# Streamed weights in DRAM by half units, and other SBUF offsets for half of the q/k weight tiles

## The chip, the cores and the metric

The kernel runs on one core of one Trainium2 chip. The metric is the device time of one execution in microseconds (us), from outside the span that the profiler records; three executions were timed, and the profile comes from another one.

## The reference, cut to what matters

One decoder block over 256 tokens of 2048 channels, in float32. Almost all of its work is products of the 256 tokens with large weight matrices:

```python
proj = x @ w_in                                   # 2048 x 13336
gq, gk, gv, gr, glr, fq, fk, fv, ff, ma, mb = jnp.split(proj, offsets, axis=-1)
q = gq.reshape(B, S, GLA_HEADS, GLA_DK) * (GLA_DK ** -0.5)
k = gk.reshape(B, S, GLA_HEADS, GLA_DK)
...
o = gla_chunked(q, k, v, log_a)                   # gated linear attention
of = fox_attention(fqh, fkh, fvh, log_f)          # softmax attention, 8 heads of 128
merged = jax.nn.sigmoid(ma) * (o @ w_branch_gla) + jax.nn.sigmoid(mb) * (of @ w_branch_fox)
x = layer_norm(ALPHA * x + merged @ w_out)
h = jax.nn.gelu(causal_dwconv(x @ w_gate)) * (x @ w_up)       # 5632 wide
x = layer_norm(ALPHA * x + h @ w_down)
x = x + jax.nn.sigmoid(x @ w_ple_gate) * (p @ w_ple_proj)
```

The change touches how the weights of these products lie in DRAM, and where the weights of `fq`, `fk`, `gq` and `gk` lie in SBUF.

## The kernel before, in words

**Units.** All large weights are laid out on the host as one tensor `wu` of units. A unit is 128 partitions x 2048 floats (1 MB) and is streamed as two halves of 128 x 1024 floats (512 KB). Units 0 to 15 are the softmax attention's q and k (`psfq`, `psfk` in the trace, one unit each in turn), 16 to 31 the linear attention's (`psq`, `psk`, two units each in turn), 32 to 135 the merge gates, v, output gate, branches and output projection, 136 to 223 the MLP's gate and up (`psg`, `psu` in turn), and the rest the down projection and the last gate.

**Precision.** A float32 product is made of three products of rounded operands: each weight half `raw` is split into `hi` (ScalarE, `copy`, L130) and `lo = raw - hi` (VectorE, L255). The activations are split likewise and lie side by side, 256 columns each.

**A q/k or gate/up unit** (`w_unit`, L314 to L342) gives 128 output channels. It runs over 16 blocks of 128 input channels. For each block it loads 128 x 128 of `hi` as weights and multiplies by 512 columns of activations (L320), then loads 128 x 128 of `lo` and multiplies by 256 columns (L325). Such a *pair* of matmuls stands 16 times in a unit. The first eight pairs take their weights from the tiles of the first half, the last eight from those of the second. In units 0 to 31 a callback (`tick`) runs after the eighth pair: it may put matmuls of the attention (`psg` L582, `pl` L622, transposes, `po`, `pa`) between the two halves. In the gate/up stage there is none, and every 14th unit (`TURN`) takes its last ten pairs in another order.

In the other stages `hi` and `lo` are the moving operand, not the weights of TensorE.

**Tiles and their offsets.** `hi` and `lo` rotate through six buffers each. A buffer has 1088 floats a partition (4352 bytes, 17 x 256), of which 1024 are used, from an offset that `place(u)` gives in floats. Both pools begin at a multiple of 256 bytes, and so do the activations `xT` and `x1T`; the offset alone sets the address modulo 256. For units 0 to 31 and the gate/up units it is 16 for `hi` and 4 for `lo` (64 and 16 bytes); for the TURN units 0 and 60 (0 and 240 bytes); elsewhere 0 and 0, but for three units.

**Streams.** SyncE issues each half's load (L251 in `prep`, L210 and L214 in `prep_s`) some three units ahead of its use, through five `raw` buffers. A unit that `park_gen` takes is loaded whole (L191), VectorE forms differences of it, GpSimd's queue writes them to the DRAM tensor `td`, and `prep_s` reads them back in a later stage. In DRAM the unit's row of 2048 floats (8 KB) of a partition is contiguous, so a half's load reads 128 runs of 4 KB, 8 KB apart.

The order of the matmuls, the splits and the loads is the program's, apart from the priorities of a scheduler; the queue of SyncE is in program order.

Of the kernel before, what the change touches and what calls it, by code (L numbers as in the profile page):

```python
# [19 lines left out]
P = 128  # L20
# [16 lines left out]


TURN = range(139, 224, 14)


def place(u):
    if 32 <= u < 136 or u >= 224:
        return 0, 0
    if 136 <= u < 139:
        return 0, 16
    return (0, 60) if u in TURN else (16, 4)


P_STAT = 5000  # L50
# [37 lines left out]
def tile_block(ctx: ExitStack, tc: tile.TileContext, wu, wfv, wpp, xT_in, x_in, pT_in, wlr,  # L88
               chan, gnorm, lng, ident_in, mask_in, cmask_in, out):
    nc = tc.nc  # L90
# [23 lines left out]
    def s8(shape, dt=F32, name=None):  # L114
        return big.tile(shape, dt, tag="S8", name=name)

    def t1(name):
        return sm.tile([P, 256], F32, tag="t1", bufs=6, name=name)
# [10 lines left out]
    def copy(o, i, scale=1.0):  # L129
        return nc.scalar.activation(o, i, AF.Copy, bias=0.0, scale=scale)  # L130
# [29 lines left out]
    hS = {}  # L160

    def lo_tile(u, name):
        o = place(u)[1]
        return rlo.tile([P, 1088], F32R, tag="lo", name=f"lo{name}")[:, o:o + 1024]

    def hi_tile(u, name):
        o = place(u)[0]
        return rhi.tile([P, 1088], F32R, tag="hi", name=f"hi{name}")[:, o:o + 1024]

    def differences(r0, r1, h, pinned=False):  # L170
# [11 lines left out]
    def park(w, i):  # L182
        for h in range(2):
            differences(w[:, 0:1024], w[:, 1024:2048], h, h == 0)
        nc.gpsimd.dma_start(td[i], w)

    def park_gen(units, lag, rest):

        for u in units:
            w = s8([P, 2048], name=f"td{parked[u]}")  # L190
            nc.sync.dma_start(w, wu[u])  # L191
            for _ in range(lag):
                yield
            park(w, parked[u])
            n = parked[u] - parked[units[0]]
            for _ in range(rest[n % len(rest)] if isinstance(rest, tuple) else rest):
                yield

    def prep_s(u):


        r0, r1 = [ring.tile([P, 1024], F32, tag="raw", bufs=5, name=f"raw{u}_{h}")
                  for h in range(2)]
        b12, b11, b22, b21 = r0[:, 0:512], r0[:, 512:1024], r1[:, 0:512], r1[:, 512:1024]
        rt = (r0, r1)
        if u in parked:
            nc.sync.dma_start(b11, wu[u, :, 512:1024])
            nc.sync.dma_start(r1, wu[u, :, 1024:2048])
            w = s8([P, 2048], name=f"td{u}")
            nc.sync.dma_start(w, td[parked[u]])  # L210
            rt = (w[:, 0:1024], w[:, 1024:2048])
        else:
            for h, r in enumerate((r0, r1)):
                nc.sync.dma_start(r, wu[u, :, h * 1024:(h + 1) * 1024])  # L214
        if dn0 <= u < dn0 + NF:
            nh = (u - dn0) // (NF // 2)
            pair = DN_ORDER[nh][(u - dn0) % (NF // 2)]
            i = DN_S[0].index(pair)
            if i % 2 == 0:
                two = s8([P, 8, 256], F32R, name=f"hS{nh}_{pair}")  # L220
                nc.sync.dma_start(two.bitcast(F32), sd[i // 2].rearrange(
                    "p (i n) -> p i n", i=8))
                hS[nh, pair], hS[nh, DN_S[0][i + 1]] = two[:, 0:4], two[:, 4:8]

        def split(src, name, e=slice(0, 1024)):
            hi = hi_tile(u, f"{u}_{name}")[:, e]
            lo = lo_tile(u, f"{u}_{name}")[:, e]
            copy(hi, src)
            nc.vector.tensor_tensor(lo, src, hi.bitcast(F32), ALU.subtract)  # L229
            return [(hi[:, o:o + 512], lo[:, o:o + 512]) for o in range(0, src.shape[1], 512)]  # L230

        x11, = split(b11, "b11", slice(512, 1024))
        x22, x21 = split(r1, "b2")
        if u not in parked:
            differences(r0, r1, 0)
        t3, t1_ = split(rt[0], "t13")
        if u not in parked:
            differences(r0, r1, 1)
        t2_, t4 = split(rt[1], "t24")
        ready[u] = [x11, x21, x22, t1_, t3, t2_, t4]  # L240

    def prep(pinned=False):
        u = n_prep[0]
        n_prep[0] += 1
        if u in s_units:
            prep_s(u)
            return
        his, los = [], []
        for h in range(2):
            raw = ring.tile([P, 1024], F32, tag="raw", bufs=5, name=f"raw{u}_{h}")  # L250
            nc.sync.dma_start(raw, wu[u, :, h * 1024:(h + 1) * 1024])  # L251
            hi = hi_tile(u, f"{u}_{h}")
            copy(hi, raw)
            lo = lo_tile(u, f"{u}_{h}")
            i = nc.vector.tensor_tensor(lo, raw, hi.bitcast(F32), ALU.subtract)  # L255
            if pinned:
                tc.keep_in_program_order(i)
            his.append(hi)
            los.append(lo)
        ready[u] = (his, los)  # L260
# [53 lines left out]
    def w_unit(ps, hi, lo, act, kts, first, last, tick=None):  # L314
# [13 lines left out]

        turn = n_used[0] - 1 in TURN
        pairs = 6 if turn else n  # L330
# [155 lines left out]
    for u in range(8):  # L486
        hi, lo = fvu[u]
        for j in range(2):
# [8 lines left out]
            for t, i, c in seq:  # L497
                o, n = fch[c]
                w, x = prods[t][i]
# [34 lines left out]
    for t in range(2):  # L534
        for c, (o, n) in enumerate(fch):
            n = min(n, 1024 - o)
# [143 lines left out]
    for n in range(16):  # L680
        h, j = n // 2, n % 2
# [115 lines left out]
    for n in range(16):  # L797
        nm, dst, sc = (("q", gq, 1.0 / 16.0), ("k", gk, 1.0))[n // 2 % 2]
        h, c = n // 4, n % 2
# [648 lines left out]
    for n in range(NF):  # L1448
# [18 lines left out]
        u = t1("up")  # L1467
# [4 lines left out]
        if pair in DN_S[0]:  # L1472
            if j == 0:
                yp = t2("yp").rearrange("p (k t) -> p k t", t=S)
            h = yp[:, j, :]
        else:
            h = y
# [4 lines left out]
        if pair in DN_S[0] and j == 1:  # L1482
            v = s_sums(yp)
            for i in range(2):
                w = sm.tile([P, 2, 256], F32R, tag="t2", bufs=6, name="hs")
# [4 lines left out]
                o = k % 2 * 1024 + 512 * i  # L1490
# [215 lines left out]
def _sst(w, orders, ssets):  # L1706


    out = []
    for nh, (order, sset) in enumerate(zip(orders, ssets)):  # L1710
        for n in order:
            b = [[w[(2 * n + j) * P:(2 * n + j + 1) * P,
                    nh * 1024 + c * 512:nh * 1024 + c * 512 + 512] for c in range(2)]
                 for j in range(2)]
            out.append(np.concatenate([b[0][1], b[0][0], b[1][1], b[1][0]] if n in sset
                                      else b[0] + b[1], 1))
    return np.stack(out)


def _fold(a):  # L1720

    return np.concatenate([a[:P], a[P:][::-1]], 0)
# [6 lines left out]
def _layout(i):  # L1729
    w_in = i["w_in"][0]  # L1730
    c = lambda nm, n: w_in[:, OFF[nm]:OFF[nm] + n]
    bg, bf = _qst(i["w_branch_gla"][0]), _qst(i["w_branch_fox"][0])
    br = [w for q in range(4) for w in (bg[4 * q:4 * q + 4], bf[2 * q:2 * q + 2])]
    gu = np.stack([_wst(i["w_gate"][0]), _wst(i["w_up"][0])], 1).reshape(2 * NF, P, 2048)
    qk = np.stack([_wst(c(n, 1024)).reshape(4, 2, P, 2048) for n in ("gq", "gk")], 1)
    m = np.concatenate([_qst(c(n, 2048)) for n in ("ma", "mb")], 0)
    wu = np.concatenate(
        [np.stack([_wst(c("fq", 1024)), _wst(c("fk", 1024))], 1).reshape(16, P, 2048), qk.reshape(16, P, 2048), m[:PSM1],
         _sst(c("gv", 2048), GV_ORDER, GV_S), _sst(c("gr", 2048), GV_ORDER, GR_S), m[PSM1:]] + br
        + [_sst(i["w_out"][0], OUT_ORDER, WO_S), gu,  # L1740
           _sst(i["w_down"][0], DN_ORDER, DN_S),
           _sst(i["w_ple_gate"][0], PG_ORDER, PG_S)], 0)
    wfv = np.concatenate([c("fv", 1024), c("glr", 16), c("ff", 8)], 1)
    wfv = wfv.reshape(8, 2, P, NS).transpose(0, 2, 1, 3)
    x = _fold(i["x"][0])
    bfo = np.zeros((P, 1), np.float32)
    bfo[:FH, 0] = i["b_forget"][0]
    chan = np.concatenate(
        [_chan(i["b_gla_lr"][0]), bfo, _chan(i["ln1_g"][0]), _chan(i["ln1_b"][0]),
         _chan(i["ln2_g"][0]), _chan(i["ln2_b"][0])]  # L1750
        + [_chan(i["conv_w"][0][j]) for j in range(3)] + [_chan(i["conv_b"][0])], 1)
    lng = np.stack([i["ln1_g"], i["ln1_b"], i["ln2_g"], i["ln2_b"]])
    s = np.arange(P)[:, None]
    t = np.arange(P)[None, :]
    masks = [s == t]
    for lev in range(1, 8):
        L = 1 << lev
        masks.append((s // L == t // L) & (s % L < L // 2) & (t % L >= L // 2))
    mask = np.stack([m if h == 0 else m.T for m in masks for h in range(2)], 1).astype(np.float32)
    caus = np.where(t <= s, 0.0, NEG).astype(np.float32)  # L1760
    cmask = np.concatenate([caus.T, caus], 1)
    return dict(wu=wu, wfv=wfv, wpp=_xst(i["w_ple_proj"][0]), xT=x.T.reshape(16, P, S).transpose(1, 0, 2),
                x=x.reshape(2, P, D), pT=_fold(i["p"][0, 0]).T.reshape(2, P, S).transpose(1, 0, 2),
                wlr=i["w_gla_lr"][0], chan=chan, gnorm=i["gla_norm_g"], lng=lng,
                ident=np.eye(P, dtype=np.float32), mask=mask, cmask=cmask)
# [20 lines left out]
```

## Time and profile before

| | |
|---|---|
| three timed executions | 1636.01 us median (1635.70 to 1637.37) |
| the profiled execution | 1635.61 us, of which the span 1633.8 us |
| TensorE matmuls, busy | 1627.3 us of the span, 8422 instructions |
| VectorE, busy | 1343.7 us |
| ScalarE, busy | 933.6 us |
| SyncE's DMA queue | 417.57 MB, 72.0% of the 16 engines' span |
| GpSimd's DMA queue | 58.73 MB, 9.0% |

How to read it: a busy share of TensorE near 100% says that matmuls stood in the array all the time, not that they ran at one rate. A matmul's recorded duration is longer than its share of the time, since matmuls are pipelined; the rate is read from the distance between the starts of successive matmuls.

### The profile page before, as it was taken

The page shows a single profiled execution, that of the slowest core. Times are in us where ns is not written, and L with a number is a line of the kernel's source. Part 1 is how long each engine was busy: PE and PEld are TensorE (multiplying, and loading weights), DVE is VectorE, ACT ScalarE, POOL GpSimd, SP SyncE. Part 2 cuts the span into 40 slices and gives each one's busy share as a digit, 9 for nine tenths or more (in the row PEclk, how much of TensorE's full clock was granted, in tenths as well). Part 3 has the DMA queues.
Part 4 walks back from the last instruction along what each step waited for, and adds up shares of the span by engine and source line. Part 5 has one row for each costly group of instructions (what it writes and reads, how often), then busy time and mean ns, then how long its engine had stood idle before and what let it go on. Part 6 is the DMA issues. An engine that isn't in the chain of part 4 may idle for free.

```text
span 1633.8 us, 23487 instructions
## 1 busy us (share of the span) xinstructions
PE 1627.3 (100%) x8422; PEld 1395.0 (85%) x8422; DVE 1343.7 (82%) x1920; ACT 933.6 (57%) x1321; POOL 93.0 (6%) x244
## 2 busy tenths in 40 slices
PE   9999999999999999999999999999999999999998
PEld 8988888888888888888898888888888888888887
DVE  7698899788989867879986887888777688988887
ACT  6655555456666653546575554665555555556554
POOL 0000000000000000000010111111110000000000
PEclk9999999999999999999999999999999999999999
DMA  9799899878898758889856887989776688899574
GB/s 328 286 371 340 295 388 352 294 261 305 305 349 299 250 191 322 299 321 389 300 187 198 323 309 284 350 305 357 280 239 222 201 285 326 305 351 355 168 261 152
DMA packets 114838, 477.81 MB, mean 292 GB/s; under 512 B 13032, under 2 KB 14320, under 8 KB 95136
## 3 DMA queue, kind: packets, MB, share of 16 engines
q1 hardware_dynamic: 105216, 417.57, 72.0%
q0 software_dynamic: 9504, 58.73, 9.0%
q8 instruction: 66, 1.08, 0.3%
q14 instruction: 52, 0.43, 0.1%
HBM read 417.53 MB, written 58.73 MB: 291 GB/s over the span
## 4 chain that ended last, share of the span: by engine, by line
PE 99%; DVE 0%; ACT 0%; DMA 0%; POOL 0%; issue 0%; SPq 0%; ACTq 0%
PE psm L1007 11%; PE dn L869 10%; PE psu L320 10%; PE psg L320 9%; PE psa L1007 5%; PE psu L325 5%; PE psg L325 5%; PE dn_p L869 4%; PE wo L869 3%; PE gr L869 3%; PE gv L869 3%; PE pg L381 3%; PE psb L1007 3%; PE fv L500 3%; PE gr_p L869 2%; PE gv_p L869 2%
## 5 line engine op out<-in xcount | busy, mean ns | idle before, releaser
L255 DVE TENSOR_TENSOR lo<-raw,hi 128x1024 fp32r<-128x1024 f32 x456 | 552.2, 1220 | 129.6 <-ACT hi L130 128.4
L130 ACT ACTIVATE hi<-raw 128x1024 fp32r<-128x1024 f32 x456 | 477.1, 1057 | 294.8 <-PE psg L320 59.3
L320 PE MATMUL psg<-x1T,hi 128*128 128x512 f32 x672 | 230.5, 389 | 0.0
L320 PE MATMUL psu<-x1T,hi 128*128 128x512 f32 x688 | 229.6, 390 | 0.0
L325 PE MATMUL psg<-x1T,lo 128*128 128x256 f32 x672 | 185.7, 276 | 0.0
L325 PE MATMUL psu<-x1T,lo 128*128 128x256 f32 x688 | 180.1, 277 | 0.0
L1007 PE MATMUL psm<-hi,xT 128*128 128x512 f32 x512 | 163.1, 392 | 0.0
L320 PEld LDWEIGHTS psu<-x1T,hi 128*128 128x128 f32 x688 | 128.7, 188 | 26.4
L320 PEld LDWEIGHTS psg<-x1T,hi 128*128 128x128 f32 x672 | 126.2, 188 | 26.1
L130 ACT ACTIVATE hi_b<-raw 128x512 fp32r<-128x512 f32 x112 | 93.6, 842 | 73.6 <-DMA raw<-in_wu_dram 19.9
L325 PEld LDWEIGHTS psg<-x1T,lo 128*128 128x128 f32 x672 | 126.1, 188 | 0.0
L325 PEld LDWEIGHTS psu<-x1T,lo 128*128 128x128 f32 x688 | 125.2, 188 | 0.6
L229 DVE TENSOR_TENSOR lo_b<-raw,hi_b 128x512 fp32r<-128x512 f32 x112 | 105.2, 953 | 18.9 <-ACT hi_b L130 18.4
L172 DVE TENSOR_TENSOR td<-td 128x512 f32<-128x512 f32 x172 | 117.9, 685 | 1.2
L1007 PEld LDWEIGHTS psm<-hi,xT 128*128 128x128 f32 x512 | 96.2, 188 | 19.6
L229 DVE TENSOR_TENSOR lo_t<-td,hi_t 128x1024 fp32r<-128x1024 f32 x86 | 101.7, 1219 | 7.6 <-ACT hi_t L130 6.9
L130 ACT ACTIVATE hi_t<-td 128x1024 fp32r<-128x1024 f32 x86 | 88.5, 1053 | 21.0 <-DMA td<-td 12.0
L1007 PE MATMUL psm<-lo,xT 128*128 128x512 f32 x256 | 99.9, 390 | 0.0
L869 PE MATMUL dn<-hi,hC 128*128 128x512 f32 x352 | 97.8, 389 | 0.0
L1007 PE MATMUL psa<-hi,oT 128*128 128x512 f32 x256 | 81.2, 392 | 0.0
L869 PEld LDWEIGHTS dn<-hi,hC 128*128 128x128 f32 x352 | 66.0, 188 | 13.7
L1464 DVE SCALAR_TENSOR_TENSOR yc<-gp,chn,yc 128x256 f32<-128x256 f32 x88 | 42.5, 483 | 21.3 <-ACT yc L1459 15.5
(414 smaller groups left out, 3140.3 us busy)
## 6 DMA issues: line engine op xcount, KB each, us to landing
raw<-in_wu_dram SPq DMA_DIRECT2D x525, 512.0 KB, 6.1
td<-in_wu_dram SPq DMA_DIRECT2D x43, 1024.0 KB, 8.7
td<-td POOLq DMA_DIRECT2D x43, 1024.0 KB, 7.7
td<-td SPq DMA_DIRECT2D x43, 1024.0 KB, 7.9
hS<-sd SPq DMA_DIRECT2D x11, 1024.0 KB, 8.7
raw<-in_wu_dram SPq DMA_DIRECT2D x43, 256.0 KB, 6.5
fvraw<-in_wfv_dram SPq DMA_DIRECT2D x13, 524.0 KB, 7.1
sd<-hs POOLq DMA_DIRECT2D x24, 256.0 KB, 6.6
```

The costliest lines, as they stand in the source:

```text
L130: return nc.scalar.activation(o, i, AF.Copy, bias=0.0, scale=scale)
L172: sub = lambda o, a, b: nc.vector.tensor_tensor(o, a, b, ALU.subtract)
L229: nc.vector.tensor_tensor(lo, src, hi.bitcast(F32), ALU.subtract)
L255: i = nc.vector.tensor_tensor(lo, raw, hi.bitcast(F32), ALU.subtract)
L320: nc.tensor.matmul(ps, lhsT=hi[i // 8][:, i % 8 * P:i % 8 * P + P], rhs=act[kts[i] // 4][:, kts[i] % 4, :], start=first and i == 0, stop=l ...
L325: nc.tensor.matmul(ps[:, 256:512], lhsT=lo[i // 8][:, i % 8 * P:i % 8 * P + P], rhs=act[kts[i] // 4][:, kts[i] % 4, 0:256], start=False, s ...
L381: nc.tensor.matmul(bs[j][:, 0:m], lhsT=x, rhs=v[:, o:o + m], start=first and i == 0, stop=last and i == 2)
L500: nc.tensor.matmul(fbk[t][c][:, 0:n], lhsT=x, rhs=w[:, o:o + n], start=kt == 0 and i == 0, stop=kt == 15 and i == 2)
L869: nc.tensor.matmul(ps[:, e], lhsT=x, rhs=w, start=k == 1, stop=k == total.get(id(ps), 3 * ns))
L1007: nc.tensor.matmul(ps[t], lhsT=x, rhs=v, start=first and i == 0 and j == 0, stop=last and i == 3 and j == 2)
L1464: nc.vector.scalar_tensor_tensor(y3, tap, cw[j], y3, ALU.mult, ALU.add)
```

## The change

Two edits. In DRAM `wu` becomes (unit, half, partition, 1024): each half is 512 KB in a row, its 128 runs of 4 KB one behind the other. Loads of halves read that, and the whole-unit load in `park_gen` reads two runs of 4 KB for each partition, 512 KB apart, where it read one of 8 KB; its destination in SBUF is the same. The load of a quarter (L210) reads 2 KB runs 4 KB apart, not 8 KB. In SBUF the tiles of units 0 to 31 that hold the second half move within their buffers: `hi` from 16 to 48 floats (64 to 192 bytes modulo 256), `lo` from 4 to 0 floats (16 to 0 bytes) where `u // 2` is even, and to 4 floats (16 bytes, as before) where it is odd. The first half's tiles stay at 16 and 4. Sizes, buffers and the order of the instructions on every engine are the same.

```diff
+SECOND = ((48, 0), (48, 4))
-def place(u):
+def place(u, h=0):
     if 32 <= u < 136 or u >= 224:
         return 0, 0
     if 136 <= u < 139:
         return 0, 16
-    return (0, 60) if u in TURN else (16, 4)
+    if u in TURN:
+        return 0, 60
+    return SECOND[u // 2 % 2] if h and u < 32 else (16, 4)
...
     def lo_tile(u, name):
-        o = place(u)[1]
+        o = place(u, name[-2:] == "_1")[1]
...
     def hi_tile(u, name):
-        o = place(u)[0]
+        o = place(u, name[-2:] == "_1")[0]
...
             w = s8([P, 2048], name=f"td{parked[u]}")
-            nc.sync.dma_start(w, wu[u])
+            nc.sync.dma_start(w.rearrange("p (h n) -> p h n", h=2), wu[u].rearrange("h p n -> p h n"))
...
-            nc.sync.dma_start(b11, wu[u, :, 512:1024])
-            nc.sync.dma_start(r1, wu[u, :, 1024:2048])
+            nc.sync.dma_start(b11, wu[u, 0, :, 512:1024])
+            nc.sync.dma_start(r1, wu[u, 1])
...
-            nc.sync.dma_start(raw, wu[u, :, h * 1024:(h + 1) * 1024])
+            nc.sync.dma_start(raw, wu[u, h])
...
+    wu = wu.reshape(-1, P, 2, 1024).transpose(0, 2, 1, 3)
```

More of the change, by code (lines that the diff above doesn't have):

```diff
@@ L213, in prep_s @@
             for h, r in enumerate((r0, r1)):
-                nc.sync.dma_start(r, wu[u, :, h * 1024:(h + 1) * 1024])
+                nc.sync.dma_start(r, wu[u, h])
         if dn0 <= u < dn0 + NF:
```

## The prediction

> **What bounds the kernel now.** I read the page first, then the clock, TensorE's waits, and the timeline of its matmuls. The page's head and the row of the engines:
>
> ```profile
> span 1633.8 us, 23487 instructions
> PE 1627.3 (100%) x8422; PEld 1395.0 (85%) x8422; DVE 1343.7 (82%) x1920; ACT 933.6 (57%) x1321; POOL 93.0 (6%) x244
> ```
>
> The clock granted, and then everything that TensorE waited for (microseconds in total, times, the longest):
>
> ```profile
> core 0: 1633.8 us, clock 0.999
> ```
>
> ```profile
> PE warm_ps L140 <- DVE warm L137: 1.2, 1, 1.2
> PE fv L500 <- ACT fvhi L130: 0.6, 1, 0.6
> ```
>
> TensorE is never starved once it has begun: 1.8 us of waits in all, both at the start, at full clock. So a load that lands earlier buys nothing, and the time can only fall where matmuls run closer together. The span lies 1.8 us below the profiled execution's own 1635.61 us, which is 0.4 us below the median of 1636.01 us; I take the sum from the former and set it on the median.
>
> The second edit concerns units 0 to 31. The views of the tiles give the durations (least, median, largest, ns) of the matmuls with `hi` (L320) and `lo` (L325) as weights, first of the softmax attention's q, then of the MLP's up:
>
> ```profile
> L320 PE MATMUL psfq<-xT,hi x128: 388/392/581, 50.9 to 143.4; 128*128 128x512 f32 x128
> L325 PE MATMUL psfq<-xT,lo x128: 275/280/367, 51.7 to 143.6; 128*128 128x256 f32 x128
> ```
>
> ```profile
> L320 PE MATMUL psu<-x1T,hi x688: 387/389/398, 846.3 to 1309.1; 128*128 128x512 f32 x172
> L325 PE MATMUL psu<-x1T,lo x688: 273/276/284, 846.6 to 1309.3; 128*128 128x256 f32 x172
> ```
>
> The same shapes, the same 64 and 16 bytes of offset, yet the median in q is 3 to 4 ns longer. The timeline shows why. I read the distance between the starts of two `hi` matmuls, which is one pair (`hi` and `lo`). Rows of the timeline of TensorE (start us, recorded us), with all rows between them left out:
>
> ```profile
> 54.56 0.40 PE L320 MATMUL psfq<-xT,hi 128*128 128x512 f32 x1
> ...
> 57.34 0.39 PE L320 MATMUL psfk<-xT,hi 128*128 128x512 f32 x1
> ...
> 74.72 0.39 PE L320 MATMUL psfq<-xT,hi 128*128 128x512 f32 x1
> ...
> 77.15 0.39 PE L320 MATMUL psfq<-xT,hi 128*128 128x512 f32 x1
> ...
> 78.02 0.71 PE L622 MATMUL pl<-fqk 128*128 128x128 f32 x3
> ...
> 78.91 0.39 PE L320 MATMUL psfq<-xT,hi 128*128 128x512 f32 x1
> ...
> 81.29 0.39 PE L320 MATMUL psfk<-xT,hi 128*128 128x512 f32 x1
> ...
> 84.01 0.39 PE L320 MATMUL psfk<-xT,hi 128*128 128x512 f32 x1
> ...
> 243.81 0.39 PE L320 MATMUL psk<-xT,hi 128*128 128x512 f32 x1
> ...
> 246.59 0.39 PE L1007 MATMUL psm<-hi,xT 128*128 128x512 f32 x1
> ...
> 862.75 0.39 PE L320 MATMUL psg<-x1T,hi 128*128 128x512 f32 x1
> ...
> 868.19 0.39 PE L320 MATMUL psu<-x1T,hi 128*128 128x512 f32 x1
> ```
>
> A whole MLP unit takes 868.19 - 862.75 = 5.44 us for 16 pairs: 340 ns. In unit 4 the first half runs at (77.15 - 74.72) / 7 = 347 ns a pair; then the attention's matmuls (`pl`) come in between the halves, and the second half runs at (81.29 - 78.91) / 7 = 340 ns, as does the next unit's first half (84.01 - 81.29 = 2.72 us for eight). So there is a **long pair** of 347 ns and a **short pair** of 340 ns, and the rate changes where other matmuls come between, or at a unit's end. The second half of unit 0 (57.34 - 54.56 = 2.78 us for eight pairs) and that of unit 31 (246.59 - 243.81 = 2.78 us) are the first and the last of the long ones. Read in this way, 22 of the 32 second halves run long (units 0 to 3, 6, 7, 10, 11, 14, 15, 18 to 20 and 23 to 31), and so do 20 of the 32 first halves.
>
> **Placement: the term of the sum.** A half of eight long pairs costs 8 x (347 - 340) = 0.055 us over short ones. The change moves the second half's weights only. All that it can remove directly is 22 x 0.055 = 1.2 us; the 20 long first halves (1.1 us) keep their offsets. What it can add directly is the ten short second halves turning long: 10 x 0.055 = 0.55 us. No row of before has weights at 192 bytes, so the sign has to be argued. That placement matters at all is shown by the TURN units, whose tiles lie at 0 and 240 bytes. Here the last pair of an MLP unit, and the first and sixth pair of the TURN unit that follows it, with nothing put in between:
>
> ```profile
> 1074.76 0.39 PE L320 MATMUL psg<-x1T,hi 128*128 128x512 f32 x1
> ...
> 1075.10 0.39 PE L320 MATMUL psu<-x1T,hi 128*128 128x512 f32 x1
> ...
> 1076.83 0.39 PE L320 MATMUL psu<-x1T,hi 128*128 128x512 f32 x1
> ```
>
> The last short pair takes 1075.10 - 1074.76 = 340 ns; with the other offsets the next five take (1076.83 - 1075.10) / 5 = 346 ns. So the rate hangs on two things: on the offset, and on something that inserted matmuls switch (call it the beat). On one beat 64 and 16 bytes are short, on the other long. From unit 4 to unit 19 the second halves alternate by pairs of units: 4, 5 short; 6, 7 long; 8, 9 short, and so on. The new table alternates in just that rhythm (`u // 2 % 2`): 192 and 0 bytes where the halves are short now, 192 and 16 where they are long. If both suit their beat, the ten stay short and the 22 become short; I take this value, -1.2 us, because 340 ns is the rate of nearly all of the gate and up units. Units 0, 1, 20, 24, 25, 28 and 29 spoil the rhythm: long now, yet given 192 and 0. If those seven stay long, 15 x 0.055 = 0.8 us goes instead.
>
> At this point the Trainium skill speaks against the change: "SBUF — State Buffer", section "Who interferes with whom", says that TensorE's reads wait for no other engine and names one port pair, shared by VectorE and GpSimd, as the only contention. By that an offset that stays a whole number of 16-byte lines would be worth nothing; the TURN unit's 346 ns after 340 ns does not agree.
>
> **The seam.** The matmuls between the halves stay, and so does the beat that they leave; the following first half lies at 64 and 16 bytes as before. I cost this at nothing; if the beat were set by the pairs' own length, first halves too would switch, between -1.1 us (all 20 short) and 12 x 0.055 = +0.7 us.
>
> **DRAM layout.** The rows of the DMA issues (KB each, median us to landing) and the waits of ScalarE for streamed halves:
>
> ```profile
> raw<-in_wu_dram SPq DMA_DIRECT2D x525, 512.0 KB, 6.1
> td<-in_wu_dram SPq DMA_DIRECT2D x43, 1024.0 KB, 8.7
> z<-x1d SPq DMA_DIRECT2D x4, 512.0 KB, 9.2
> praw<-in_wpp_dram SPq DMA_DIRECT2D x4, 512.0 KB, 6.8
> ppk<-ppd SPq DMA_DIRECT2D x2, 512.0 KB, 7.2
> ```
>
> ```profile
> ACT hi L130 <- DMA raw<-in_wu_dram: 53.4, 59, 2.5
> ```
>
> The runs stay 4 KB, 525 loads. No `wu` load of before is contiguous; the nearest rows are `ppk` (512 KB in a row: 7.2 us) and `z`, `praw` and `raw` (4 KB runs 8 KB apart: 9.2, 6.8 and 6.1). Contiguous lies inside the others, so I take no change, bounded by 6.1 to 9.2 us. A gain only shortens ScalarE's 53.4 us of waits, which TensorE does not see. The cover is the distance from a split to its use; in the first units it is thinnest at unit 4:
>
> ```profile
> 71.33 1.20 DVE L255 TENSOR_TENSOR lo<-raw,hi 128x1024 fp32r<-128x1024 f32 x1
> ```
>
> ```profile
> 74.72 0.19 PEld L325 LDWEIGHTS psfq<-xT,lo 128*128 128x128 f32 x1
> ```
>
> The split ends at 71.33 + 1.20 = 72.53 and the weight load begins at 74.72: 2.2 us. Four shortened halves before it bring the need forward by 0.2 us, so nothing is late next. If a load took 9.2 for 6.1 us there, 0.9 us would come through. The 43 whole-unit loads get twice as many runs: they should land between 8.7 us and two halves' 12.2. Behind them VectorE's differences wait, and behind those the splits; the loads are issued two units (11 us) ahead, so at worst about 1 us of waiting, inside those 2.2 us. I cost both at nothing.
>
> **The sum.** 1635.61 - 1.2 = 1634.4 us for a profiled execution, 1636.01 - 1.2 = 1634.8 us for the median.
>
> **The rivals.**
> 1. *Placement does nothing for the second halves* (or helps as many as it hurts): 1636.0 us. For it: the same offsets show both rates. Against: the TURN unit.
> 2. *The beat goes too*: all 42 long halves become short, 42 x 0.055 = 2.3 us: 1633.7 us. Against: the tables leave first halves where they are.
> 3. *The offsets suit the wrong beat*: ten halves turn long, the 22 stay: 1636.6 us. For it: 192 bytes has no row.
> 4. *The loads grow and starve TensorE* in the q/k stage. Rows of the stretches (us, then TensorE, its loads, VectorE, ScalarE and GpSimd busy; clock, DMA share, GB/s):
>
> ```profile
> 50.94:149.33 98.39, 98.25 (x583) 86.80 (x581) 84.00 (x153) 58.97 (x113) 4.98 (x9) 1.00 0.88 319
> 149.33:246.58 97.25, 97.25 (x582) 86.42 (x582) 87.00 (x146) 53.09 (x94) 5.64 (x9) 1.00 0.92 349
> ```
>
> The 16 DMA engines are at 0.92 of their time there. If the new addresses made transfers slower by over 1 / 0.92 - 1 = 9%, the stage would run at their pace. At 15% the second stretch would need 1.06 of its time, 97.25 x 0.058 = 5.6 us more: 1641.6 us. Against: `ppk` lands like the others.
>
> **How the numbers follow.** Chances: forecast (-0.8 to -1.2 us) 0.45; rival 1 0.28; rival 2 0.13; rival 3 0.09; rival 4 0.05. About 0.2% (3.3 us) is what a measurement of this kernel can tell from no change. All placement cases lie inside it, so "same" is very likely. Faster by more would need rival 2 and a further 1 us elsewhere: 0.04. Slower by more is rival 4: 0.05. The range goes from rival 2 to rival 3, each with a little for the timed executions' own spread of 1635.70 to 1637.37: 1633.4 to 1637.0 us.
>
> **What would show it.** Right: the median of `lo` in `psfq` falls from 280 toward 276, second halves at 2.72 us for eight pairs, first halves as before, still no waits of TensorE. Wrong: second halves at 2.78 us (rivals 1, 3), first halves short too (rival 2), or waits of TensorE for splits and a DMA share near 1.0 before 247 us (rival 4).

## The result, and the profile after

The changed kernel takes **1633.68 us** (median of 22 executions, 1633.18 to 1634.27) where the kernel before takes 1635.85 us (22 executions, 1635.27 to 1637.39): an estimated ratio of 0.9985 (the two medians alone give 0.9987), with a 95% interval of 0.9980 to 0.9991. That is 2.2 us, inside the stated range and inside 0.2%, but nearly twice the 1.2 us that was forecast. It is the size of the second rival, to which the prediction gave 0.13.

The head of the page after, and what TensorE waited for:

```profile
span 1631.6 us, 23487 instructions
PE 1625.7 (100%) x8422; PEld 1394.5 (85%) x8422; DVE 1343.3 (82%) x1920; ACT 934.1 (57%) x1321; POOL 93.9 (6%) x244
```

```profile
PE warm_ps L143 <- DVE warm L140: 1.2, 1, 1.2
```

TensorE still waits for nothing once it has begun, at the same work. The view of the softmax attention's q (least, median, largest duration in ns; three lines were added above them, so L320 and L325 are now L323 and L328):

```profile
L323 PE MATMUL psfq<-xT,hi x128: 389/389/585, 51.0 to 142.7; 128*128 128x512 f32 x128
L328 PE MATMUL psfq<-xT,lo x128: 276/276/369, 51.8 to 143.0; 128*128 128x256 f32 x128
```

The medians went from 392 to 389 and from 280 to 276 ns, which are the MLP's. The timeline, again with the rows between left out: the second half of unit 0, then unit 4's first half, then its second half behind the attention's matmuls:

```profile
54.64 0.39 PE L323 MATMUL psfq<-xT,hi 128*128 128x512 f32 x1
...
57.37 0.39 PE L323 MATMUL psfk<-xT,hi 128*128 128x512 f32 x1
...
74.44 0.39 PE L323 MATMUL psfq<-xT,hi 128*128 128x512 f32 x1
...
76.83 0.39 PE L323 MATMUL psfq<-xT,hi 128*128 128x512 f32 x1
...
78.58 0.40 PE L323 MATMUL psfq<-xT,hi 128*128 128x512 f32 x1
...
79.62 0.39 PE L323 MATMUL psfq<-xT,hi 128*128 128x512 f32 x1
...
80.98 0.39 PE L323 MATMUL psfk<-xT,hi 128*128 128x512 f32 x1
```

Unit 0: 57.37 - 54.64 = 2.73 us for eight pairs, where it was 2.78. Unit 4's first half, whose tiles did not move: (76.83 - 74.44) / 7 = 341 ns a pair, where it was 347. Its second half: three pairs at (79.62 - 78.58) / 3 = 347 ns right behind the inserted matmuls, and then four at (80.98 - 79.62) / 4 = 340 ns. So a half still begins long where something comes in between, and then *falls back* to the short rhythm. Read over all 64 halves, none is long any more: not the 22 second ones, and not the 20 first ones either, whose tiles did not move. The time above 340 ns a pair, without the pairs that hold inserted matmuls, went from 1.18 to 0.34 us in the second halves and from 1.02 to 0.01 us in the first. The two stretches of the q/k stage:

```profile
51.04:149.33 98.29, 98.15 (x587) 86.93 (x585) 83.91 (x153) 59.66 (x114) 4.99 (x9) 1.00 0.88 328
149.33:244.73 95.40, 95.40 (x578) 85.03 (x577) 86.29 (x146) 52.79 (x94) 5.66 (x9) 1.00 0.92 348
```

From the first q/k pair to the first merge-gate matmul it is 98.29 + 95.40 = 193.69 us, where it was 195.64: 2.0 of the span's 2.2 us. The DMA share is what it was. The loads (median us to landing) and ScalarE's waits for them:

```profile
raw<-in_wu_dram SPq DMA_DIRECT2D x525, 512.0 KB, 5.2
td<-in_wu_dram SPq DMA_DIRECT2D x43, 1024.0 KB, 8.1
```

```profile
ACT hi L133 <- DMA raw<-in_wu_dram: 20.4, 26, 2.3
```

Halves land 0.9 us earlier than before, and ScalarE waits 20.4 us for them in place of 53.4.

### The profile page after: what moved, and what is told of

It is laid out like the page before. It is cut to its first block, busy times and chain, and to the rows that moved or that the text cites. A ratio compares the mean times of both kernels' runs of the same rounds, so it can differ in the third digit from the quotient of the medians.

```text
span 1631.6 us, 23487 instructions
## 1 busy us (share of the span) xinstructions
PE 1625.7 (100%) x8422; PEld 1394.5 (85%) x8422; DVE 1343.3 (82%) x1920; ACT 934.1 (57%) x1321; POOL 93.9 (6%) x244
## 4 chain that ended last, share of the span: by engine, by line
PE 99%; DVE 0%; ACT 0%; POOL 0%; issue 0%; ACTq 0%
PE psm L1010 11%; PE dn L872 10%; PE psu L323 10%; PE psg L323 9%; PE psa L1010 5%; PE psu L328 5%; PE psg L328 5%; PE dn_p L872 4%; PE wo L872 3%; PE gr L872 3%; PE gv L872 3%; PE fv L503 3%; PE pg L384 3%; PE psb L1010 3%; PE gr_p L872 2%; PE gv_p L872 2%
## 5 line engine op out<-in xcount | busy, mean ns | idle before, releaser
L323 PE MATMUL psg<-x1T,hi 128*128 128x512 f32 x672 | 230.5, 389 | 0.0
L323 PE MATMUL psu<-x1T,hi 128*128 128x512 f32 x688 | 229.6, 389 | 0.0
L328 PE MATMUL psg<-x1T,lo 128*128 128x256 f32 x672 | 185.5, 276 | 0.0
L328 PE MATMUL psu<-x1T,lo 128*128 128x256 f32 x688 | 179.9, 276 | 0.0
L323 PEld LDWEIGHTS psu<-x1T,hi 128*128 128x128 f32 x688 | 128.6, 188 | 26.5
L323 PEld LDWEIGHTS psg<-x1T,hi 128*128 128x128 f32 x672 | 126.2, 188 | 26.1
L328 PEld LDWEIGHTS psg<-x1T,lo 128*128 128x128 f32 x672 | 126.1, 188 | 0.0
L328 PEld LDWEIGHTS psu<-x1T,lo 128*128 128x128 f32 x688 | 125.2, 188 | 0.6
```

Source lines behind the costliest of these rows:

```text
L323: nc.tensor.matmul(ps, lhsT=hi[i // 8][:, i % 8 * P:i % 8 * P + P], rhs=act[kts[i] // 4][:, kts[i] % 4, :], start=first and i == 0, stop=l ...
L328: nc.tensor.matmul(ps[:, 256:512], lhsT=lo[i // 8][:, i % 8 * P:i % 8 * P + P], rhs=act[kts[i] // 4][:, kts[i] % 4, 0:256], start=False, s ...
```

## The experiments

All kernels compute the whole block. Three theories were put to the test. **Own rate** (the prediction's): a half's rate follows from its own offsets and from a beat that the inserted matmuls set. **Drawn back**: the beat is a phase that the stream of pairs carries along; at 64 and 16 bytes the long and the short phase both last, at the new offsets the long one decays (they draw the stream back), and what follows takes over the phase. Matmuls that come in between two pairs can switch the phase; such an insertion is called a kick below. **Loads**: the quicker loads made the pairs short.

**1. The DRAM layout alone** (`e1_layout_only`).

```diff
-    return SECOND[u // 2 % 2] if h and u < 32 else (16, 4)
+    return 16, 4
```

> DRAM by half units as in the changed kernel, all q/k tiles at 64 and 16 bytes as before. Own-rate theory (each half's rate comes from its own offsets and the beat that inserted matmuls set) and drawn-back theory (the beat is a phase that the stream of pairs carries from half to half; at 64 and 16 bytes both phases persist, at 192 bytes the long one decays): both leave about 20 long first halves and 22 long second halves, so q/k from its first pair to the first merge-gate matmul takes 195.6 us as before, and the time is 1635.4 to 1635.9 us (at most 0.4 us off at the start). Load theory (quicker loads made the pairs short): no long halves, 193.7 us for q/k, about 1633.7 us.

Measured: 1635.65 us (11 executions), beside 1635.87 before on the same chip; ratio 0.9996 (0.9987 to 1.0005), no difference. The loads' row and the first and last rows of the stage:

```profile
raw<-in_wu_dram SPq DMA_DIRECT2D x525, 512.0 KB, 5.3
```

```profile
50.85 0.48 PE L323 MATMUL psfq<-xT,hi 128*128 128x512 f32 x1
```

```profile
246.28 0.39 PE L1010 MATMUL psm<-hi,xT 128*128 128x512 f32 x1
```

The loads are as quick as in the changed kernel, and q/k takes 246.28 - 50.85 = 195.4 us; 19 first and 19 second halves are long. The load theory falls. There is a hint beside it: unit 6's second half came out short here, where it was long in before, and from there to unit 20 every half that was long in before is short and the other way round (unit 8's second half is long, unit 10's short). The pattern belongs to the stream's history, not to the units.

**2. The offsets alone** (`e2_offsets_only`): the kernel before, with `SECOND` and the four lines that use it.

> DRAM as before, second halves at the changed offsets. Drawn-back theory: no long half left, first halves short too, 193.7 to 193.8 us for q/k, 1633.8 to 1634.1 us. Own-rate theory: 20 first halves stay long, 194.4 us, about 1634.7 us. Load theory: 42 long halves, 195.6 us, about 1635.8 us.

Measured: 1633.98 us (11 executions); ratio 0.9986 (0.9978 to 0.9995). First and last rows of the stage:

```profile
51.39 0.48 PE L325 MATMUL psfq<-xT,hi 128*128 128x512 f32 x1
```

```profile
245.08 0.40 PE L1012 MATMUL psm<-hi,xT 128*128 128x512 f32 x1
```

193.69 us, as in the changed kernel to the last digit, with no long half, first halves included. In q/k the placement is the whole effect, and the own-rate theory, which kept first halves long, falls here.

**3 and 4. One placement for all second halves** (`e3_all_192_0`, `e4_all_192_16`): `SECOND[u // 2 % 2]` becomes `(48, 0)`, and in the other kernel `(48, 4)`.

> As the changed kernel, but every second half at 192 and 0 bytes, none at 192 and 16. Drawn-back theory: 192 bytes for hi is what lets the long phase decay, so all halves end short and the time is within 0.4 us of 1633.7. Own-rate theory with two beats: the halves on the other beat (units 2, 3, 6, 7, 10, 11, 14, 15, 18, 19) turn long, 10 x 0.055 = 0.55 us more, and with the first halves behind them 1.1 us more: 1634.2 to 1634.8 us.

> As the changed kernel, but every second half at 192 and 16 bytes. Drawn-back theory: all halves end short, within 0.4 us of 1633.7. Own-rate theory with two beats: units 4, 5, 8, 9, 12, 13, 16, 17 turn long in their second halves, 0.45 to 0.9 us more: 1634.1 to 1634.6 us.

Measured: 1633.65 us, ratio 0.9984 (0.9975 to 0.9993), and 1633.47 us, ratio 0.9983 (0.9974 to 0.9992), 11 executions each. The alternation in the table is not needed. One half escaped, unit 6's second in `e3_all_192_0`:

```profile
90.92 0.40 PE L323 MATMUL psfq<-xT,hi 128*128 128x512 f32 x1
...
93.37 0.39 PE L323 MATMUL psfk<-xT,hi 128*128 128x512 f32 x1
93.72 0.39 PE L323 MATMUL psfk<-xT,hi 128*128 128x512 f32 x1
...
97.80 0.39 PE L323 MATMUL psfk<-xT,hi 128*128 128x512 f32 x1
```

(93.37 - 90.92) / 7 = 350 ns to its end, and the next unit, after one pair, runs at (97.80 - 93.72) / 12 = 340 ns. So 192 and 0 can hold a long rhythm of its own now and then.

**5. New offsets in even units only** (`e5_even_units`): `if h and u < 32 and u % 2 == 0`.

> As the changed kernel, but only units of even number have the new offsets in their second half; odd units lie at 64 and 16 bytes throughout. Drawn-back theory: units 4 to 22, where matmuls come in between the halves of even units only, are short in all halves but for the first few pairs after them (before: 11 long first and 9 long second halves among these units), odd ones too, since they take over the short phase; from unit 23 on the kick comes in odd units, which now have nothing that draws back, so long halves reappear there and end in the next even second half. Own-rate theory: odd second halves are long where they were long before (7, 11, 15, 19).

Measured: 1634.50 us, one execution. Units 23 and 24 in its timeline:

```profile
196.24 0.40 PE L323 MATMUL psk<-xT,hi 128*128 128x512 f32 x1
...
198.68 0.39 PE L323 MATMUL psq<-xT,hi 128*128 128x512 f32 x1
...
201.45 0.40 PE L323 MATMUL psq<-xT,hi 128*128 128x512 f32 x1
...
202.16 0.39 PE L323 MATMUL psq<-xT,hi 128*128 128x512 f32 x1
...
204.20 0.39 PE L323 MATMUL psq<-xT,hi 128*128 128x512 f32 x1
```

Unit 23's second half, at the old offsets, stays long behind the kick (349 ns), unit 24's first half goes on at 346 ns, and its second half falls to 340 ns after two pairs. From unit 9 to unit 22 all halves are short, among them the second halves of 11, 15 and 19, at the old offsets and long in before. One miss: the second halves of units 6 and 30 (192 and 16) held a rhythm of 353 to 354 ns to the end, so units 7 and 31 were long too. The draw fails in some places.

**6. New offsets in the first halves** (`e6_first_halves`): `if not h and u < 32`.

> The new offsets in the first halves of units 0 to 31, 64 and 16 bytes in the second. Drawn-back theory: every first half ends short; the kick between the halves of units 4, 6, 8, 10, 12, 14, 16, 18 now always meets a short phase and leaves a long one that lasts to the end of the half, so second halves of 8, 12 and 16 are long too, which were short before; the next first half ends it. Own-rate theory: first halves short, second halves as before, short in 4, 5, 8, 9, 12, 13, 16, 17.

Measured: 1634.50 us, one execution. Units 8 and 9:

```profile
98.72 0.39 PE L323 MATMUL psfq<-xT,hi 128*128 128x512 f32 x1
...
101.10 0.39 PE L323 MATMUL psfq<-xT,hi 128*128 128x512 f32 x1
...
103.77 0.39 PE L323 MATMUL psfq<-xT,hi 128*128 128x512 f32 x1
...
105.85 0.40 PE L323 MATMUL psfk<-xT,hi 128*128 128x512 f32 x1
...
106.56 0.39 PE L323 MATMUL psfk<-xT,hi 128*128 128x512 f32 x1
...
108.60 0.39 PE L323 MATMUL psfk<-xT,hi 128*128 128x512 f32 x1
```

First half 340 ns, second 347 ns (short in before), and the next first half is back at 340 ns after two pairs. Units 12 and 16 do the same, as the drawn-back theory said. Two first halves (21 and 23) stayed long at the new offsets, and unit 6's kick left the stream short.

**7 and 8. Another stage: the TURN units taken out** (`e7_no_turn`: `TURN = ()`; `e8_no_turn_192`: also `SECOND[u // 2 % 2] if h`, so gate and up units have the new offsets too). If phases last, a stage with no kicks at all should show it best.

> As the changed kernel, without the TURN units: units 139, 153 and so on to 223 are in the ordinary order at 64 and 16 bytes. The seven TURN units take about 5.53 us each, the other gate and up units 5.44. If nothing else happens: 7 x 0.09 = 0.65 us less, 1633.0 us. Drawn-back theory: with nothing that draws back, a long phase that comes up somewhere in the stage (it starts from the products before it) stays: up to 85 units x 0.11 = 9 us more, 1643 us; if it comes up every 14 units and is turned back by the next such event, about half.

> As the last kernel, and every second half of the gate and up units lies at 192 and 0 or 16 bytes as in q/k. Drawn-back theory: a long phase ends in the next second half at the latest, so all units take 5.44 to 5.50 us, and the time is 1632.9 to 1633.5 us. Own-rate theory: half of the second halves turn long, 43 x 0.055 = 2.4 us more than without: about 1635.5 us.

Measured: 1642.00 us (6 executions), ratio 1.0036 (1.0024 to 1.0049), and 1633.03 us (10 executions), ratio 0.9981 (0.9971 to 0.9990). The view of `psu` without TURN at the old offsets:

```profile
L323 PE MATMUL psu<-x1T,hi x688: 392/392/392, 844.5 to 1315.6; 128*128 128x512 f32 x172
L328 PE MATMUL psu<-x1T,lo x688: 280/280/281, 844.7 to 1315.9; 128*128 128x256 f32 x172
```

and with the new ones:

```profile
L323 PE MATMUL psu<-x1T,hi x688: 389/389/394, 844.9 to 1307.0; 128*128 128x512 f32 x172
L328 PE MATMUL psu<-x1T,lo x688: 276/276/280, 845.1 to 1307.3; 128*128 128x256 f32 x172
```

All 688 `hi` matmuls took 392 ns, least and largest: a long phase that came in with the first unit lasted for half a millisecond at 64 and 16 bytes. Outside the TURN units it is the same placement that runs short throughout in before. There the first MLP unit is a TURN unit and begins at 347 ns too, and the unit behind it runs at 340: the TURN units, at 0 and 240 bytes and in another order, leave the stream in the short phase. Whether the offsets or the order does it, no run tells.

**9. The offset of `lo` alone** (`e9_lo_only`): `(16, 0) if h and u < 32`.

> As the changed kernel, but in the second halves of units 0 to 31 hi stays at 64 bytes and only lo moves, from 16 to 0. If the distance between lo and the activations does it: no long halves but for the first pairs after inserted matmuls, q/k from its first pair to the first merge-gate matmul in 193.8 us. If it takes hi at 192: long halves as before, about 20 first and 20 second ones, 195.4 to 195.6 us.

Measured: 1637.28 us, one execution, q/k 196.3 us: 13 first and 27 second halves long, the latter with median pairs of 348 to 353 ns. So it takes `hi` at 192 bytes; with `lo` at 0 beside `hi` at 64, q/k takes longer than in both kernels (196.3 us; 195.6 in before), more than either theory allowed for. The rest of that one execution's excess lies ahead of q/k, which began at 52.4 us, not 50.9, and says nothing of the offsets.

**10. Eight other placements** (`e10_table`).

```diff
+TABLE = {4: (0, 0), 6: (0, 4), 8: (32, 0), 10: (32, 4), 12: (56, 4), 14: (40, 4), 16: (16, 36),
+         18: (48, 36)}
...
+    return TABLE.get(u, (48, 4)) if h and u < 32 else (16, 4)
```

> Second halves at 192 and 16 bytes, except in eight units in which matmuls come in between the halves, with one placement each (hi, lo in bytes modulo 256): unit 4 at 0 and 0, 6 at 0 and 16, 8 at 128 and 0, 10 at 128 and 16, 12 at 224 and 16, 14 at 160 and 16, 16 at 64 and 144, 18 at 192 and 144. Each enters short and is kicked, so a placement that draws back shows a few long pairs and then 340 ns, one that does not shows 347 ns or more to the end of the half. Drawn-back theory says no more than that some do and that the next second half (192 and 16) ends what is left: no long half from 20 to 22. If only 192 and 16 or 0 can do it, seven of the eight stay long, 18 perhaps not.

Measured: 1633.85 us, one execution. All eight halves stayed long, with median pairs of 347 to 353 ns. Unit 8 (128 and 0) and the two halves behind it:

```profile
103.00 0.39 PE L324 MATMUL psfq<-xT,hi 128*128 128x512 f32 x1
...
105.46 0.40 PE L324 MATMUL psfk<-xT,hi 128*128 128x512 f32 x1
...
106.17 0.39 PE L324 MATMUL psfk<-xT,hi 128*128 128x512 f32 x1
...
108.25 0.39 PE L324 MATMUL psfk<-xT,hi 128*128 128x512 f32 x1
...
108.59 0.39 PE L324 MATMUL psfk<-xT,hi 128*128 128x512 f32 x1
...
110.97 0.39 PE L324 MATMUL psfq<-xT,hi 128*128 128x512 f32 x1
```

351 ns, then 347 ns at 64 and 16, then 340 ns at 192 and 16. After four of the eight (units 8, 10, 14, 18) the old offsets went on long, after the other four short. Of what was tried only `hi` at 192 with `lo` at 0 or 16 draws back; each of the others was seen once.

**11 and 12. All second halves at the new offsets, and a single one, without TURN** (`e11_all_drawn`: no TURN, `(48, 4) if h` for q/k, gate and up; `e12_one_half`: no TURN, `SECOND[u // 2 % 2] if h and (u < 32 or u == 139)`, which moves one half of the MLP's 170).

> Second halves of q/k and of gate and up at 192 and 16 bytes, no TURN units: the two best pieces together. Drawn-back theory: 1632.8 to 1633.1 us, that is 0.6 us (seven TURN units of 0.09 us) under the changed kernel and no different from the kernel without TURN and with 192 and 0 or 16 bytes (1633.03).

> As the kernel without TURN units that took 1642.0 us, but a single half of the MLP's 85 units, the second half of the first one (unit 139), lies at 192 and 16 bytes. Drawn-back theory: its pairs fall to the short rhythm within the half and all 84 units behind it, at 64 and 16 bytes as before, stay short: 1633.0 to 1633.3 us. Own-rate theory: one half of 170 gains its 0.055 us, 1641.9 us.

Measured: 1633.11 us (11 executions), ratio 0.9986 (0.9977 to 0.9995), and 1632.96 us (10 executions), ratio 0.9983 (0.9974 to 0.9992). The first MLP unit of `e12_one_half`, with the tile that moved as its second half, and the whole stage:

```profile
844.49 0.39 PE L323 MATMUL psu<-x1T,hi 128*128 128x512 f32 x1
...
846.91 0.39 PE L323 MATMUL psu<-x1T,hi 128*128 128x512 f32 x1
...
847.60 0.39 PE L323 MATMUL psu<-x1T,hi 128*128 128x512 f32 x1
...
849.98 0.39 PE L323 MATMUL psg<-x1T,hi 128*128 128x512 f32 x1
```

```profile
L323 PE MATMUL psu<-x1T,hi x688: 389/389/394, 844.5 to 1306.6; 128*128 128x512 f32 x172
```

The unit begins at (846.91 - 844.49) / 7 = 346 ns; from the second pair of the moved tile on it is (849.98 - 847.60) / 7 = 340 ns, and all 84 units behind it, at the old offsets, stay there. One tile moved by 128 bytes is worth 1642.00 - 1632.96 = 9.0 us. The two were timed on different chips, but the stage itself tells the same: `psu` runs from 844.5 to 1315.6 us in `e7_no_turn` and from 844.5 to 1306.6 here, 471.1 and 462.1 us. Against the changed kernel these two should save the seven TURN units' excess (their pairs took 5.53 us a unit, not 5.44, so 0.6 us), and from the first merge-gate matmul to the end their profiles take 1386.2 us where the changed kernel's takes 1386.9. That a whole execution is faster than the changed kernel's is not shown: the ratios against before (0.9986 and 0.9983, beside 0.9985) have intervals that overlap, and neither was timed beside it.

## Why the prediction was right or wrong, point by point

- **The bound: right.** Once it has begun, TensorE waits for nothing before or after; only the distance between matmuls could move.
- **DRAM layout: right in its cost, wrong in its size.** The loads were taken as unchanged; they land in 5.2 us, not 6.1, and the whole-unit loads in 8.1, not between 8.7 and 12.2. The bound left out a row: the prediction says that no `wu` load of before is contiguous, but the whole-unit load is (`td`, 1 MB in a row); half of its 8.7 us, 4.4 us, as the lower bound would have let in 5.2. All this is worth nothing that can be measured (experiment 1), since no wait of TensorE hangs on them.
- **That placement sets the rate: right.** The prediction weighed against it the rule of the Trainium skill, "SBUF — State Buffer", section "Who interferes with whom", that only the port pair shared by VectorE and GpSimd causes contention. The prediction's own reading of that rule, that offsets in whole 16-byte lines are worth nothing, does not hold here: experiments 7 and 12 differ by 9.0 us.
- **Second halves, -1.2 us: too large.** All 22 became short, but 0.34 us remains in the few long pairs behind each kick, so the term measured 1.18 - 0.34 = 0.8 us.
- **Two beats, one offset for each: wrong.** The table's alternation and the trace's were a coincidence: either offset alone serves (experiments 3 and 4), and with all offsets as before the trace's own alternation turned over (experiment 1). That the 22 second halves became short was forecast rightly, but for this wrong reason, and in that the forecast was lucky. The seven units that "spoil the rhythm" became short as well.
- **The seam, costed at nothing: the step that failed.** It held that inserted matmuls leave the beat and that the following first half keeps its own rate. The beat is a phase of the stream. The second half draws it to the short one, and the next first half, itself unmoved, takes that over: another 1.0 us. The bound written there (-1.1 us, all 20 short) was what happened, and with it the second rival, which had been marked down because "the tables leave first halves where they are".
- **The sum.** 0.8 + 1.0 us by the pairs, 2.0 us by the stage's length, 2.2 us by the span and the medians. The stage's 2.0 us exceed the pairs' sum because the pairs that hold kicks became shorter too. The last 0.2 us lie outside q/k and have no cause shown; the part behind q/k, 1633.8 - 246.59 = 1387.2 us before and 1386.9 after, is as short with either edit alone (1386.8 and 1386.7).
- **What a measurement can tell: too coarse.** The prediction put the limit at 0.2% (3.3 us); with 22 executions of each kernel the interval leaves out 1 at 2.2 us.

What stays open: what the phase physically is, why some kicks leave the stream short (unit 6 in experiments 1 and 6), and why 192 bytes failed in five halves of experiments 3, 5 and 6 (350 to 354 ns).

## What to carry to other kernels

Where an engine is busy all the time, read the distance between successive starts, unit by unit, before calling its time fixed: two rates in one shape of work are a lever that no wait shows. Ask whether the slow rate is a property of the place or a condition that the stream carries from place to place; a stretch without disturbance, as in experiments 7 and 12, told the two apart here. A fix then needs to act only at a place where the stream can be brought out of the condition, and its gain is counted over all that follows, not over what it touches.

## What was not expected of the hardware

- A stream of weight load and matmul pairs (512 and 256 columns, float32r) has at least two lasting rhythms at the same offsets, 340 and 347 ns a pair; left alone, each lasted for all of the gate and up units behind it (experiments 7 and 12).
- The offset of the weights in their buffers (given here in bytes modulo 256) decided which rhythms last. `hi` at 192 with `lo` at 16 or 0 let the long one decay in one to four pairs, but for five halves; eight other placements, each seen once, ran at 347 to 353 ns.
- 512 KB loads of 128 runs of 4 KB landed in 5.1 to 5.4 us (median of each of twelve kernels) when the runs follow one another in DRAM, and in 6.1 us (two kernels) when they lie 8 KB apart, with the DMA engines at 0.9 of their time in q/k either way. Loads beside them whose layout did not change came earlier too: `td<-td` landed in 6.5 us, not 7.9.
